# Output projection, h2 copies, last gates and samples' transposes moved in a one-layer decoder step

## The chip, the cores and the metric

The kernel runs on one core of one Trainium2 chip. The metric is the device time of one execution in microseconds (us), lower is better. The engines are TensorE (PE; PEld is its weight load), VectorE (DVE), ScalarE (ACT), GpSimd (POOL) and SyncE (SP), which here only issues transfers.

## What is computed

One decoder layer for 576 tokens: 512 of a prompt and 8 samples of 8 tokens, with a model width of 2048.

```python
mod = (jax.nn.silu(c) @ w_ada + b_ada).reshape(c.shape[0], 6, D_MODEL)
shift1, scale1, gate1, shift2, scale2, gate2 = [mod[:, k] for k in range(6)]
h = modulate(rmsnorm(x, norm1_g), shift1, scale1)
proj = h @ w_in                       # 2048 -> x_lru | y_gate | B | C | x_sc, 1024 each
...
xc, new_lru_buf = causal_dwconv(x_lru, lru_buf, lru_conv_w)
rec, h_last = rglru(xc + lru_conv_b, h0, lru_wa, lru_ba, lru_wx, lru_bx, lru_lambda)
out_lru = rec * jax.nn.gelu(y_gate)
conv_out, new_sc_buf = causal_dwconv(sc_c * sc_x, sc_buf, sconv_w)
out_sc = sc_b * conv_out
mix = jnp.concatenate([rmsnorm(out_lru, gnorm_lru_g), rmsnorm(out_sc, gnorm_sc_g)], axis=-1) @ w_out
x = x + gate1[:, None, :] * mix
h2 = modulate(rmsnorm(x, norm2_g), shift2, scale2)
x = x + gate2[:, None, :] * peer(h2, peer_wq, peer_sub_keys, peer_u, peer_v)
...                                   # then a final RMSNorm
```

`peer` is a product-key layer: 8 heads score 128 x 128 keys, each token takes the 16 best of 16384 single-neuron experts for each head, and the sum of their outputs, weighted by a softmax, is added.

## The kernel before

Everything is kept with channels on the partitions: a tensor of width 2048 is 16 blocks `k` of 128 channels by 576 tokens, and a matmul takes the tokens in two halves of 288 (`HT`). All large products are made in three parts, to come near full precision: an operand is split into a high part (`hi`, a rounding copy on ScalarE) and a low part (`lo`, the difference, on VectorE or GpSimd), and high x high, high x low and low x high are added up. `hv[0]` and `hv[1]` are the split activations, first of h, later of the mixers' outputs, later of h2. Weights are streamed by halves of 8 blocks, with two buffers each for the raw, high and low form; the low form of the weights is made on GpSimd. One projection of 128 output channels (`project`, `mm3`) is 16 blocks x 3 parts x 2 halves = 96 matmuls into a pair of PSUM banks; there are two such pairs (tag `pp`).

The first stage works in this order. The adaLN modulation is computed by units of 4 matmul calls (`ada_mm`, profile line L185; `ada_out`, L195), which `ada_turn` strews between projections. The head of group A has 8 mixers `i` (128 channels each): projections x and y, convolution, two gate products (`lru_gate(i, 0)` and `lru_gate(i, 1)`, L431, tiles `pg`, made into `tr` and `ti` by ScalarE), the scan (`lru`, `gate`). Then the square sums of group A (`sqa_g`, tag L216), projections c, s and b of the 8 mixers of group B (`pp_c`, `pp_s`, `pp_b`), each with its follow-up on ScalarE or VectorE (`sc_c`, `sc_x` at L482 to L491, `sc_b` at L497 to L499). `norm_stats` sums the squares over the channels on TensorE (L224, tile `pc_g`) and makes the factors on VectorE (L139 to L145, tile `rc_g`); `spread` puts them on all partitions by TensorE (L232, `st_g`). Group A's outputs are scaled (L545) and split while group B is still worked on; group B's are scaled at L557 and split at L241 and L242 (`hhi`, `hlo`). Then come the 16 projections of `w_out` (`pp_o`), the residual x1 and the statistics of x1 (`pc_n`).

h2 is made in four quarters of 4 blocks. For each quarter: `modulate` (multiply on VectorE or GpSimd, high part on ScalarE at L270, low part on VectorE at L271), 24 matmuls of the first query projection (`qa`), and 32 matmuls that transpose the quarter back to tokens on the partitions (L608, tile `wide`, four PSUM banks), which ScalarE copies to `h2s` (L611) for a store to `h2d`. The next query projection takes one of the first three banks of `wide`.

In this first stage TensorE's order is the order of the program. The orders of the other engines are set by a planner when the program is built; `tc.high_priority()` raises what stands in it ahead of other work that is ready. Later, from the last query head on, every engine keeps the order of the program.

Then come the query projections, the choice of experts, and two long loops on TensorE over the 84 most used key rows: the U loop (L1270) and the V loop (L1290; 84 steps of 4 columns `kq`, 12 matmuls a column). The experts outside those rows are gathered by row on GpSimd's queue and summed on VectorE (L1159, L1185), and their sums stored to `accd`. `finish_b` finishes the 64 sample tokens in six pieces, which `fplan` puts at places (step, column) in the V loop: load of the samples' rows (`tokb`, L1346, and `x2b`); transposes on TensorE (`ph`, L1353) with the residual behind them; sum of squares; statistics; spreading; last multiplication and store of the samples' y (L1364). `last` is step 75 of 84. At step 79 the prompt's rows (`tok`) are loaded, which the last four steps transpose and add (L1294). In the V loop SP also loads weight blocks of a later step (L831) and blocks of x (`xf`, L1301).

Of the kernel before, what the change touches and what calls it, by code (L numbers as in the profile page):

```python
# [21 lines left out]
HT = T // 2  # L22
NCTX = 1 + NB
W = 1024
KW = 8
# [47 lines left out]
def r32(ap):  # L73
    return ap.bitcast(F32)


def build(ctx, tc, A, O, dbg=None):
    nc = tc.nc
    V, S, PE, G = nc.vector, nc.scalar, nc.tensor, nc.gpsimd
# [4 lines left out]
    ws = ctx.enter_context(tc.tile_pool(name="ws", bufs=1))  # L84
# [24 lines left out]
    def lo_engine(share):  # L109

        turn[0] += 1
        return G if turn[0] * share // 8 != (turn[0] - 1) * share // 8 else V

    def stream_w(src, nm, share=8):
        his, los = [], []
        for hf in range(2):
            raw = ws.tile([128, 8, 128], F32, name=f"raw_{nm}_{hf}", tag="wraw", bufs=2)
            nc.sync.dma_start(raw, src[:, 8 * hf:8 * hf + 8, :])
            hi = ws.tile([128, 8, 128], F32R, name=f"whi_{nm}_{hf}", tag="whi", bufs=2)
            S.activation(hi, raw, AF.Copy)  # L120
            lo = ws.tile([128, 8, 128], F32R, name=f"wlo_{nm}_{hf}", tag="wlo", bufs=2)
            lo_engine(share).tensor_sub(lo, raw, r32(hi))  # L122
            his.append(hi)
            los.append(lo)
        return his, los

    def mm3(outs, his, los, movs, ks=range(KD)):

# [111 lines left out]
    def split(hi, lo, src, eng=V):  # L240
        S.activation(hi, src, AF.Copy)  # L241
        eng.tensor_sub(lo, src, r32(hi))  # L242
# [135 lines left out]
    o = big.tile([128, KD, T], F32, name="o", tag="big")  # L378

    def project(src, nm):  # L380
        his, los = stream_w(src, nm)
        p = pp.tile([128, 2, 512], F32, name=f"pp_{nm}", tag="pp")
        mm3([p[:, 0, :HT], p[:, 1, :HT]], his, los, movs)
        return p
# [39 lines left out]
    def lru_gate(i, j):  # L424
        xc = xcs[i]
        hl = LN // 2
        dst, g, hc = (wt("tr", i), gw[0], i) if j == 0 else (wt("ti", i), gw[1], KW + i)
        for q in range(2):
            pg = pst.tile([128, 512], F32, name=f"pg{i}_{hc}_{q}", tag="st")
            for z in (slice(0, 64), slice(64, 128)):  # L430
                PE.matmul(pg[z, :hl], g[z, i, :], xc[z, q * hl:(q + 1) * hl], start=True, stop=True)  # L431
            S.activation(dst[:, q * hl:(q + 1) * hl], pg[:, :hl], AF.Tanh, scale=0.5, bias=hb[:, hc:hc + 1])
        gts[i, j] = dst
# [26 lines left out]
    def gate_act(i, halves):  # L460
        ygs[i] = wk.tile([128, T], F32, name=f"yg{i}", tag="yg", bufs=2)
        for a, p in enumerate(halves):
            S.activation(ygs[i][:, a * HT:(a + 1) * HT], p, AF.Gelu_apprx_tanh)
# [8 lines left out]
    def sc_c(i, p):  # L472
        c = wk.tile([128, T], F32, name=f"scc{i}", tag="yg", bufs=2)
        S.activation(c.rearrange("p (a b) -> p a b", a=2), p[:, :, :HT], AF.Copy)
        sc_t[i] = c
# [28 lines left out]
    def ada_turn(n, keep=7):  # L504

        for a in pend:
            ada_out(*a)
        pend.clear()
        for _ in range(min(n, len(todo) - keep)):
            a = todo.pop(0)  # L510
            ada_mm(*a)
            if a[2] == 3:
                pend.append(a[:2])
                break
# [4 lines left out]
    for i in range(KW):  # L519
        if i + 1 < KW:  # L520
            lru_conv(i + 1, px)
        if i + 2 < KW:
            px = project(A["w_in"][i + 2], f"x{i + 2}")
            ada_turn(1)
        lru_gate(i, 0)
        if i + 1 < KW:
            py = project(A["w_in"][KW + i + 1], f"y{i + 1}")
            gate_act(i + 1, [py[:, a, :HT] for a in range(2)])
        lru_gate(i, 1)
        lru(i)  # L530
        gate(i)
        ada_turn(1)
    st = []
    for i in range(KW):
        square_sum(o[:, i, :], i, st, "g0")
    for i in range(KW):
        sc_c(i, project(A["w_in"][24 + i], f"c{i}"))
        if i == 0:
            spread = norm_stats(st, W, "g0")
        ada_turn(2)  # L540
        if i == 0:
            R = spread()
            st = []
            for k in range(KW):
                V.scalar_tensor_tensor(o[:, k, :], o[:, k, :], cols[:, C_GN + k:C_GN + k + 1], R, op0=ALU.mult, op1=ALU.mult)  # L545
        sc_x(i, project(A["w_in"][32 + i], f"s{i}"))
        ada_turn(2)
        sc_b(i, project(A["w_in"][16 + i], f"b{i}"))
        ada_turn(2)
        square_sum(o[:, KW + i, :], i, st, "g1")  # L550
    for k in range(KW):
        split(hv[0][:, k, :], hv[1][:, k, :], o[:, k, :], G if k % 2 else V)
    spread = norm_stats(st, W, "g1")
    ada_turn(2)
    R = spread()
    for k in range(KW, KD):
# [9 lines left out]
    st = []  # L566
    g1 = mods[2]
    for k in range(KD):
        p = project(A["w_out"][k], f"o{k}")
        xk = wk.tile([128, T], F32, name=f"xk{k}", tag="yg", bufs=2)  # L570
        nc.sync.dma_start(xk, A["xt"][:, k, :])
        V.scalar_tensor_tensor(x1[:, k, :HT], p[:, 0, :HT], g1[:, k, 0:1], xk[:, :HT], op0=ALU.mult, op1=ALU.add)
        V.scalar_tensor_tensor(x1[:, k, HT:NP], p[:, 1, :NX], g1[:, k, 0:1], xk[:, HT:NP], op0=ALU.mult, op1=ALU.add)
        V.tensor_tensor(s3(x1[:, k, NP:]), s3(p[:, 1, NX:HT]), ctx_b(g1, k), op=ALU.mult)
        V.tensor_add(x1[:, k, NP:], x1[:, k, NP:], xk[:, NP:])
        nc.sync.dma_start(x1d[:, k, :], x1[:, k, :])
        square_sum(x1[:, k, :], k, st, "n2")
        S.activation(x1[:, k, :NP], x1[:, k, :NP], AF.Copy, scale=mods[4][:, k, 0:1])
        V.tensor_tensor(s3(x1[:, k, NP:]), s3(x1[:, k, NP:]), ctx_b(mods[4], k), op=ALU.mult)
        ada_turn(1)  # L580
# [21 lines left out]
    for q in range(4):  # L602
        modulate(x1, R, 4, 3, 4 * q, 4, "h2")
        mm3(pq0, *w_q, movs, range(4 * q, 4 * q + 4))
        for i in range(NA // 128):
            for k in range(4):
                for p in range(2):
                    PE.matmul(wide[:, i, k * 128:(k + 1) * 128], hv[p][:, 4 * q + k, i * 128:(i + 1) * 128], idr,  # L608
                              start=p == 0, stop=p == 1)
        t = adap.tile([128, 4, 512], F32, name=f"h2s{q}", tag="wa")  # L610
        S.activation(t, wide, AF.Copy)  # L611
        for i in range(NA // 128):
            nc.sync.dma_start(h2d[i * 128:(i + 1) * 128, q * 512:(q + 1) * 512], t[:, i, :])
    pe1.close()
# [968 lines left out]
            room[m, kq] = PIECE / 2 - 0.75 * steps[m][4] - 0.38  # L1583
    tot, run_ = sum(room.values()), 0.0
    fb = finish_b()
    fplan = {(last + 1, 2), (last + 2, 0), (last + 2, 2), (last + 2, 3), (last + 3, 1), (last + 3, 3)}
    NT = len(uses)
    cost = [FULL_ROWS if j < NU + bound[0] else 1.0 for j in range(NV0, NT)]
    sums = [sum(cost[:j + 1]) for j in range(len(cost))]
# [189 lines left out]
```

## Time and profile before

| | |
|---|---|
| time, median of 3 runs | 3421.0 us (3416.03 to 3427.66) |
| profiled execution | 3418.08 us, of which the span of its instructions 3416.3 us |
| granted TensorE clock, mean | 0.961 |
| TensorE busy | 3196.4 us (94%) |
| VectorE busy | 2164.3 us (63%) |
| ScalarE busy | 1083.4 us (32%) |
| GpSimd busy | 1752.5 us (51%) |
| DMA | 868.17 MB, mean 254 GB/s |

A row of the groups or of the order of time names line, engine, operation, tiles (written<-read) and count; what stands in square brackets or behind an arrow is the idle time of that engine just before, and what ended it. A row of the waits gives the total in us, how often, and the longest. A row of the stretches gives for each engine the busy us and the number of instructions.

### The profile page before, as it was taken

The numbers are of one execution on the slowest core, as the hardware profiler recorded it, in microseconds if no ns is written. First come the engines' busy times: TensorE is split into PE (matmuls) and PEld (weight loads), VectorE is DVE, ScalarE is ACT, GpSimd is POOL, SyncE is SP. The second block draws the span as 40 slices with busy tenths as digits, with TensorE's granted clock in tenths as the row PEclk, the third lists the DMA queues.
The fourth block names the chain that finished last, engine by engine and source line by source line (L and its number), as shares of the span: only waits on it lengthen the run. The fifth ranks groups of instructions, "written<-read, shape, count | busy, mean of one in ns | idle before, by whom it ended". The sixth has DMA issues, their size and how long they took to land.

```text
span 3416.3 us, 47510 instructions
## 1 busy us (share of the span) xinstructions
PE 3196.4 (94%) x17641; PEld 2710.3 (79%) x17641; DVE 2164.3 (63%) x3246; ACT 1083.4 (32%) x1665; POOL 1752.5 (51%) x993
## 2 busy tenths in 40 slices
PE   5899999989979999989999999998999999999887
PEld 2698788989969988878888888876888777777776
DVE  5355522143346887968786787766677777787735
ACT  3234311132232232315555555522322222222122
POOL 4233233344333336646555566566767766676742
PEclk8899999999989999989999999998999999999988
DMA  9644466634442137759986979899999988898954
GB/s 337 231 139 139 160 208 205 216 114 128 130 138 71 66 102 255 263 186 366 340 302 259 376 284 370 317 365 334 369 386 368 368 297 330 301 393 297 337 170 148
DMA packets 304029, 868.17 MB, mean 254 GB/s; under 512 B 36618, under 2 KB 80522, under 8 KB 255658
## 3 DMA queue, kind: packets, MB, share of 16 engines
q1 hardware_dynamic: 165152, 390.35, 33.5%
q0 software_dynamic: 62896, 386.64, 29.0%
q10 hardware_dynamic: 75744, 88.09, 7.3%
q8 instruction: 139, 2.28, 0.3%
q14 instruction: 98, 0.80, 0.1%
HBM read 864.69 MB, written 68.90 MB: 273 GB/s over the span
## 4 chain that ended last, share of the span: by engine, by line
PE 39%; DMA 9%; DVE 8%; issue 5%; POOL 3%; ACT 0%; SPq 0%; POOLq 0%; ACTq 0%; DVEq 0%
PE pu L1270 19%; PE pv L1290 15%; PE gbank L1463 3%; DMA v<-v,rows 3%; DMA gsb<-gd 2%; DMA actr<-actd 2%; DVE u L1159 2%; DVE accB L1185 2%; DMA raw<-v 1%; POOL xlo L843 1%; DVE flags L1000 1%; POOL u L1131 1%; DMA h2r<-h2d,tok 0%; DVE oh L728 0%; PE pv L1294 0%
## 5 line engine op out<-in xcount | busy, mean ns | idle before, releaser
L843 POOL TENSOR_TENSOR xlo<-raw,xhi 128x1024 fp32r<-128x1024 f32 x336 | 818.4, 2447 | 643.9 <-ACT xhi L842 637.0
L842 ACT ACTIVATE xhi<-raw 128x1024 fp32r<-128x1024 f32 x336 | 354.1, 1059 | 922.9 <-PE pv L1290 466.1
L1159 DVE SCALAR_TENSOR_TENSOR u<-u,hT 128x2048 f32<-128x2048 f32 x211 | 479.5, 2284 | 242.5 <-DMA u<-u,rows 242.0
L1185 DVE SCALAR_TENSOR_TENSOR accB<-v,dots,accB 128x2048 f32<-128x2048 f32 x205 | 482.4, 2353 | 156.3 <-DMA v<-v,rows 154.5
L1290 PE MATMUL pv<-ahi,xhi 128*128 128x512 f32 x1344 | 540.9, 402 | 31.3 <-DVE acc L1312 24.2
L1290 PE MATMUL pv<-ahi,xlo 128*128 128x512 f32 x1344 | 538.3, 401 | 17.0 <-POOL xlo L843 16.9
L1270 PE MATMUL pu<-hhi,xhi 128*128 128x512 f32 x1344 | 543.4, 404 | 4.3 <-ACT xhi L842 4.3
L1270 PE MATMUL pu<-hhi,xlo 128*128 128x512 f32 x1344 | 529.8, 394 | 7.5 <-POOL xlo L843 7.5
L1290 PE MATMUL pv<-alo,xhi 128*128 128x512 f32 x1344 | 534.8, 398 | 0.0
L1270 PE MATMUL pu<-hlo,xhi 128*128 128x512 f32 x1344 | 531.4, 395 | 0.0
L1290 PEld LDWEIGHTS pv<-ahi,xhi 128*128 128x128 f32 x1344 | 257.8, 192 | 93.1 <-issue 16.7
L1290 PEld LDWEIGHTS pv<-ahi,xlo 128*128 128x128 f32 x1344 | 257.3, 191 | 82.8 <-POOL xlo L843 22.8
L1270 PEld LDWEIGHTS pu<-hhi,xlo 128*128 128x128 f32 x1344 | 254.8, 190 | 67.8 <-POOL xlo L843 10.4
L1290 PEld LDWEIGHTS pv<-alo,xhi 128*128 128x128 f32 x1344 | 258.0, 192 | 58.6
L1270 PEld LDWEIGHTS pu<-hhi,xhi 128*128 128x128 f32 x1344 | 255.6, 190 | 57.5 <-ACT xhi L842 5.6
L1270 PEld LDWEIGHTS pu<-hlo,xhi 128*128 128x128 f32 x1344 | 255.5, 190 | 50.1
L1131 POOL DMA_INDIRECT v<-v,rows x211 | 249.2, 1181 | 58.3 <-issue 32.5
L1131 POOL DMA_INDIRECT u<-u,rows x211 | 221.3, 1049 | 72.1 <-DVE u L1159 32.3
L1457 ACT ACTIVATE op<-op,it 128x128 f32<-128x128 f32 x512 | 154.3, 389 | 0.0
L185 PE MATMUL ada<-wa,cpad 128*32 128x512 f32 x768 | 112.5, 691 | 42.9 <-DMA wa<-w_ada 42.9
L1463 PEld LDWEIGHTS gbank<-wr,op 128*128 128x128 f32 x1024 | 135.5, 193 | 18.7 <-ACT op L1457 8.0
L122 POOL TENSOR_TENSOR wlo_q<-raw_q,whi_q 128x1024 fp32r<-128x1024 f32 x28 | 67.4, 2407 | 146.1 <-ACT whi_q L120 146.1
(477 smaller groups left out, 5574.9 us busy)
## 6 DMA issues: line engine op xcount, KB each, us to landing
wa<-w_ada SPq DMA_DIRECT2D x96, 1024.0 KB, 6.4
raw<-ut SPq DMA_DIRECT2D x168, 512.0 KB, 5.8
raw<-v SPq DMA_DIRECT2D x336, 256.0 KB, 8.0
actd<-act ACTq DMA_DIRECT2D x84, 256.0 KB, 7.1
gd<-stg ACTq DMA_DIRECT2D x64, 336.0 KB, 8.8
actr<-actd ACTq DMA_DIRECT2D x21, 1024.0 KB, 21.3
gsb<-gd ACTq DMA_DIRECT2D x21, 1024.0 KB, 26.2
raw_o<-w_out SPq DMA_DIRECT2D x32, 512.0 KB, 3.8
```

Of the source, the lines that this page charges most:

```text
L122: lo_engine(share).tensor_sub(lo, raw, r32(hi))
L185: PE.matmul(acc[32 * g:32 * g + 32, :], cpad[:, 4 * kq + g, :], w[:, g, :], start=kq == 0, stop=kq == 3)
L842: S.activation(hi, raw, AF.Copy)
L843: G.tensor_sub(lo, raw, r32(hi))
L1000: V.scalar_tensor_tensor(fl, i1, perm[:, x:x + 1], fl, op0=ALU.is_equal, op1=ALU.add)
L1131: G.indirect_dma_start(out=out, out_offset=None, in_=src, in_offset=bass.IndirectOffsetOnAxis(ap=idx, axis=0), bounds_check=NE * 128 - 1, ...
L1159: V.scalar_tensor_tensor(r, r, 1.0, st["h"], op0=ALU.mult, op1=ALU.mult, accum_out=dots[i][:, j:j + 1])
L1185: V.scalar_tensor_tensor(st["a"], r, dots[i][:, j:j + 1], st["a"], op0=ALU.mult, op1=ALU.add)
L1270: PE.matmul(pu, st[:, kk, :], movA[mv](k), start=k == 0 and a == 0, stop=k == KD - 1 and a == 2)
L1290: PE.matmul(pv, st, mv, start=first and j == 0 and a == 0, stop=last and not end and j == SG - 1 and a == 2)
L1457: S.activation(ops[:, j0 + j, :], ops[:, j0 + j, :], AF.Copy, scale=it[2][:, b * 4 + j:b * 4 + j + 1])
L1463: PE.matmul(pg[:, j * L:(j + 1) * L], ops[:, j0 + j, :], wr[:, j0 + j, :], start=True, stop=True)
```

## The change

Four places are changed.

1. The last mixer of group A: between its two gate products now stand an adaLN unit and projection c0. In group B, every projection s now comes directly after c and one adaLN turn; the statistics of group A, which stood behind c0, now stand behind s0.
2. The first two output projections are made by halves. The halves over group A's blocks (`out_half(0, 0)`, `out_half(1, 0)`) now stand ahead of the statistics of group B and between them and the spreading; the halves over group B's blocks follow when the loop over `w_out` comes to them. `half_w` is the half of `stream_w`, taken out of it.
3. The copy of the transposed h2 is made by pairs of PSUM banks, each after its 16 matmuls, under `tc.high_priority()`, instead of all four banks after 32.
4. In `fplan` the second to the sixth piece of the samples' end are moved: (last + 2, 0) to (last + 2, 3), (last + 2, 2) to (last + 3, 1), (last + 2, 3) to (last + 3, 3), (last + 3, 1) to (last + 4, 1), (last + 3, 3) to (last + 4, 3).

```diff
+    def half_w(src, nm, hf, share=8):
+        raw = ws.tile([128, 8, 128], F32, name=f"raw_{nm}_{hf}", tag="wraw", bufs=2)
+        nc.sync.dma_start(raw, src[:, 8 * hf:8 * hf + 8, :])
+        hi = ws.tile([128, 8, 128], F32R, name=f"whi_{nm}_{hf}", tag="whi", bufs=2)
+        S.activation(hi, raw, AF.Copy)
+        lo = ws.tile([128, 8, 128], F32R, name=f"wlo_{nm}_{hf}", tag="wlo", bufs=2)
+        lo_engine(share).tensor_sub(lo, raw, r32(hi))
+        return hi, lo
...
             gate_act(i + 1, [py[:, a, :HT] for a in range(2)])
+        else:
+            ada_turn(1)
+            pc0 = project(A["w_in"][24], "c0")
         lru_gate(i, 1)
         lru(i)
         gate(i)
-        ada_turn(1)
+        if i + 1 < KW:
+            ada_turn(1)
...
-        sc_c(i, project(A["w_in"][24 + i], f"c{i}"))
+        sc_c(i, project(A["w_in"][24 + i], f"c{i}") if i else pc0)
+        ada_turn(2)
+        sc_x(i, project(A["w_in"][32 + i], f"s{i}"))
         if i == 0:
             spread = norm_stats(st, W, "g0")
         ada_turn(2)
...
-        sc_x(i, project(A["w_in"][32 + i], f"s{i}"))
-        ada_turn(2)
         sc_b(i, project(A["w_in"][16 + i], f"b{i}"))
...
+    def out_half(k, hf):
+        hi, lo = half_w(A["w_out"][k], f"o{k}", hf)
+        mm3([p_out[k][:, i, :HT] for i in range(2)], (hi, hi), (lo, lo), movs, range(8 * hf, 8 * hf + 8))
+
+    p_out = [pp.tile([128, 2, 512], F32, name=f"pp_o{k}", tag="pp") for k in range(2)]
+    out_half(0, 0)
     spread = norm_stats(st, W, "g1")
+    out_half(1, 0)
     ada_turn(2)
     R = spread()
...
-        p = project(A["w_out"][k], f"o{k}")
+        if k < 2:
+            out_half(k, 1)
+            p = p_out[k]
+        else:
+            p = project(A["w_out"][k], f"o{k}")
...
+        t = adap.tile([128, 4, 512], F32, name=f"h2s{q}", tag="wa")
         for i in range(NA // 128):
             for k in range(4):
                 for p in range(2):
                     PE.matmul(wide[:, i, k * 128:(k + 1) * 128], hv[p][:, 4 * q + k, i * 128:(i + 1) * 128], idr,
                               start=p == 0, stop=p == 1)
-        t = adap.tile([128, 4, 512], F32, name=f"h2s{q}", tag="wa")
-        S.activation(t, wide, AF.Copy)
+            if i % 2:
+                with tc.high_priority():
+                    S.activation(t[:, i - 1:i + 1, :], wide[:, i - 1:i + 1, :], AF.Copy)
...
-    fplan = {(last + 1, 2), (last + 2, 0), (last + 2, 2), (last + 2, 3), (last + 3, 1), (last + 3, 3)}
+    fplan = {(last + 1, 2), (last + 2, 3), (last + 3, 1), (last + 3, 3), (last + 4, 1), (last + 4, 3)}
```

More of the change, by code (lines that the diff above doesn't have):

```diff
@@ L114, in stream_w @@
     def stream_w(src, nm, share=8):
[L115 to L124, printed above, removed]
-        return his, los
+        his, los = zip(*[half_w(src, nm, hf, share) for hf in range(2)])
+        return his, los
+    def half_w(src, nm, hf, share=8):
[6 more added lines that the diff above has]
+        return hi, lo
     def mm3(outs, his, los, movs, ks=range(KD)):
```

## The prediction, made before the changed kernel was run

> **What bounds the kernel now.** I read the page first, then TensorE's waits, then the busy time of each engine over short stretches, then the order of instructions inside those stretches.
>
> ```profile
> PE 3196.4 (94%) x17641; PEld 2710.3 (79%) x17641; DVE 2164.3 (63%) x3246; ACT 1083.4 (32%) x1665; POOL 1752.5 (51%) x993
> ```
>
> TensorE is busy 94% of the span and its instructions run in the order in which they are written, so an edit gains what it takes out of TensorE's idle time and out of the slow clock that follows idle time. The waits of TensorE in the first stage, between 357 and 1019.5 us, longest first (total, times, longest):
>
> ```profile
> PE wide L608 <- ACT h2s L611: 9.0, 1, 9.0
> PE pc_g L224 <- DVE sqa_g L216: 8.7, 2, 6.8
> PE pg L431 <- ACT tr L432: 5.1, 1, 5.1
> ...
> PE wide L135 <- ACT h2s L611: 2.0, 1, 2.0
> PE pp_o L135 <- POOL hlo L242: 1.9, 1, 1.9
> PE st_g L232 <- DVE rc_g L145: 1.5, 1, 1.5
> PE ada L185 <- DMA wa<-w_ada: 1.3, 1, 1.3
> ```
>
> The change touches `pg`, both `pc_g`, `st_g`, `pp_o` and both `wide` rows: 28.2 us. The stretches where they lie: from mixer 7's first gate to projection s0, from b7 to the last split of group B, from the first quarter's transposes of h2 to the next query projection, and, near the end, from V step 76 to its neighbour's last column. PEclk is the granted clock, the counts beside PE are of matmuls:
>
> ```profile
> core 0: us, PE busy (x) PEld busy (x) DVE busy (x) ACT busy (x) POOL busy (x), PEclk, DMA share, GB/s
> 357.10:387.00 29.90, 23.05 (x148) 17.67 (x149) 18.65 (x29) 9.45 (x16) 7.57 (x3) 0.83 0.37 123
> 728.30:756.40 28.10, 17.61 (x110) 17.05 (x110) 21.49 (x27) 8.83 (x14) 9.44 (x5) 0.80 0.15 50
> 982.50:1018.70 36.20, 25.24 (x168) 24.86 (x167) 12.12 (x13) 14.86 (x16) 20.04 (x13) 0.76 0.33 111
> 3272.00:3297.20 25.20, 18.22 (x70) 15.57 (x69) 6.94 (x6) 3.27 (x3) 4.27 (x2) 0.66 0.40 101
> 383.60:387.00 3.40, 3.40 (x18) 2.13 (x11) 0.67 (x4) 0.61 (x2) 0.15 (x1) 0.50 0.65 196
> 3303.50:3325.80 22.30, 22.30 (x98) 18.16 (x98) 9.36 (x9) 4.47 (x5) 9.06 (x5) 1.00 0.82 260
> ```
>
> In the first four rows TensorE stands still for 6.9, 10.5, 11.0 and 7.0 us, and the granted clock is 0.66 to 0.83. The last row is the same engine undisturbed: clock 1.00, 22.30/98 = 0.228 us a matmul. So a wait costs itself and then work at half clock. The four parts of the change answer to the first four rows in order.
>
> **The last gates behind a projection.** For mixer 7 the two gate products stood one behind the other; now one adaLN unit and projection c0 stand between them.
>
> ```profile
> 355.83 1.23 PE L431 MATMUL pg<-xc,g_lru_wa 64*64 64x300 f32 x8 [0.96 <-ACT ti L432]
> 362.14 2.27 PE L431 MATMUL pg<-xc,g_lru_wx 64*64 64x300 f32 x8 [5.08 <-ACT tr L432]
> 364.34 1.94 PE L185 MATMUL ada<-wa,cpad 128*32 128x512 f32 x8
> ...
> 381.21 1.28 PE L224 MATMUL pc_g<-ones,sqa_g 128*128 128x1 f32 x10 [1.81 <-DVE sqa_g L216]
> 382.42 2.52 PE L185 MATMUL ada<-wa,cpad 128*32 128x512 f32 x16
> ```
>
> Between the end of `ada` (366.28) and the idle time before `pc_g` (379.40) lies c0: 13.1 us for 96 matmuls, 0.137 each. Moved ahead of the second gate, it covers the 5.08 us wait for `tr`. The squares then have s0 (another 13.1) to arrive in, so the 1.81 before `pc_g` goes as well. With them goes slow clock: the second gate's 2.27 against 1.23 (1.0), 8 adaLN matmuls in 1.94 where 16 take 2.52 (0.7), half of the 3.4 us at 0.50 (1.7). That is 10.3. The moved adaLN unit takes its weight load ahead of c0's on SP's queue; that costs nothing while loads run ahead (the last row of the waits: 1.3 us in the whole stage), and 1.3 if not.
>
> What is late next: s0 now comes before the statistics, and its follow-up on VectorE is written ahead of theirs.
>
> ```profile
> 400.09 0.46 DVE L482 TENSOR_TENSOR cx<-pp_s,scc 128x288 f32<-128x288 f32 x1 [6.44 <-PE pp_s L135]
> ...
> 403.88 1.71 DVE L491 SCALAR_TENSOR_TENSOR cv<-cx,cols,cv 128x592 f32<-128x592 f32 x2
> ```
>
> It lasts 5.5 us (400.09 to 405.59). From the end of s0, TensorE has `pc_g` (1.3) and 16 adaLN matmuls (2.5), then wants the factors: at 3.8. If they queue behind the 5.5 and then need their own 1.5 (the `st_g` row), they come at 7.0: a new wait of 3.2, with all of b0 behind it, and 1.7 to 3.4 of slow clock. Part: 10.3 - 3.2 - 3.4 = 3.7 to 10.3; I take 6, near the queued case, as VectorE keeps its order.
>
> The Trainium skill's page "TensorE: Matmul & The Clock Gate", section "HAM oscillation — how this bites in real kernels", lets only idle gaps over about 3.4 us throttle the clock; here 1.81 us was followed by 3.4 us at 0.50, so the trace doesn't bear the limit out. By that rule the 3.2 us would cost no clock and this part would be 7.1, 1 us more than taken.
>
> **Output projection begun with the first mixer.** Two half projections, 96 matmuls, move ahead of and behind group B's square statistics; the sum of the work is unchanged.
>
> ```profile
> 729.17 3.56 DVE L242 TENSOR_TENSOR hlo<-o,hhi 128x576 fp32r<-128x576 f32 x2
> ...
> 741.82 2.28 DVE L557 SCALAR_TENSOR_TENSOR o<-o,cols,R_g 128x576 f32<-128x576 f32 x3 [2.91 <-ACT R_g L236]
> 744.01 1.42 DVE L242 TENSOR_TENSOR hlo<-o,hhi 128x576 fp32r<-128x576 f32 x2
> ...
> 750.05 4.82 DVE L557 SCALAR_TENSOR_TENSOR o<-o,cols,R_g 128x576 f32<-128x576 f32 x2
> ```
> ```profile
> 749.81 2.57 POOL L122 TENSOR_TENSOR wlo_o<-raw_o,whi_o 128x1024 fp32r<-128x1024 f32 x1 [3.09 <-ACT whi_o L120]
> 752.34 1.92 POOL L242 TENSOR_TENSOR hlo<-o,hhi 128x576 fp32r<-128x576 f32 x1
> ```
>
> Before: the second split on GpSimd (ends 754.26) is of k = 13, which TensorE waits for after 13 x 6 + 2 = 80 matmuls; the 112 left of o0 and o1 end at 754.3 + 15.3 = 769.6. After: the first half (48 x 0.137 = 6.6) starts at 728.3, the last of its splits is there at 732.7, so it ends about 734.9, just as `pc_g` could start before (728.3 + 6.8). `pc_g` to 736.2, the second half to 742.8, the spreading about 1.3 (10 short matmuls, by the 2.52 of 16 above), and the scaling of group B starts at about 744.7 instead of 741.8: the factors are 2.9 later. From there VectorE needs between 10.3 us (8 scalings of 0.76, 6 splits of 0.71, the undisturbed rows) and what it took before, about 14.5 (741.82 to the splits behind 754.87). The last split is done at 755.0 to 759.2; one k of matmuls (0.8) and the last half projection (6.6) end at 762.4 to 766.6, a gain of 3.0 to 7.2. TensorE idles three to four microseconds before k = 8, so up to 3.4 of slow clock falls into the last half: 0 to 7. Against the better end: the second half frees a weight buffer at 742.8, so a weight subtraction of 2.57 on GpSimd runs into the first scaling. I take 3.
>
> That GpSimd stalls VectorE is in the rows: two scalings took 4.82 us under GpSimd's 2.57 + 1.92, three took 2.28 with it idle. "SBUF — State Buffer" of the Trainium skill, section "Who interferes with whom", gives the cause, an exclusive port pair, and this trace agrees; it speaks against this part, since by it the fast end (7.2) isn't to be had.
>
> **The h2 copies by pairs of banks.** Four copies of four banks become eight of two, written ahead in priority.
>
> ```profile
> 989.50 0.71 ACT L270 ACTIVATE hhi<-m_h,mod 128x512 fp32r<-128x512 f32 x1
> 992.15 0.72 ACT L270 ACTIVATE hhi<-m_h,mod 128x512 fp32r<-128x512 f32 x1 [1.94 <-POOL m_h L269]
> 992.78 1.86 ACT L611 ACTIVATE h2s<-wide 128x2048 f32<-128x2048 f32 x1
> ```
> ```profile
> 1001.50 2.38 POOL L122 TENSOR_TENSOR wlo_q<-raw_q,whi_q 128x1024 fp32r<-128x1024 f32 x1
> ```
>
> The first copy had its transposes at about 982.5, but stood in ScalarE's queue behind the high parts of k = 12 and 13. TensorE did its 24 matmuls of the second quarter (3.3) and then stood for the 9.0. A pair is ready two microseconds earlier than all four banks, so I put its copy behind k = 12 (990.2 + 0.9 = 991.1) and the other behind k = 13: TensorE goes on 3.5 us sooner. The 2.0 before the next query projection goes too, which needs only a bank of the first pair, and about 1.7 of the clock lost behind it: 7 in all. If the queue stays as it is, half a copy (0.9) and the 2.0 are left: 3. If the copies pass the whole queue, the next bound is the weight part at 1003.88, without which the next projection (1018.7 before) cannot start: 15.
>
> **The samples' transposes later.** `ph` moves behind three columns of the V loop (36 matmuls), the later steps with it.
>
> ```profile
> 3279.00 7.09 PE L1353 MATMUL ph<-ident,tokb 64*128 64x64 f32 x32 [6.98 <-DMA tokb<-accd]
> ```
> ```profile
> 3274.18 0.54 SPq L1346 DMA_DIRECT2D tokb<-accd x1
> ```
> ```profile
> DMA to landing us min/median/max: 4.8/4.8/4.8
> ```
>
> The rows it needs land at 3274.18 + 4.8 = 3278.98. Three columns from 3272.0 take 36 x 0.228 = 8.2, so `ph` starts at 3280.2, 1.2 us after the landing: the 6.98 goes. So does slow clock: up to half of the 7.09, and of the stretch's other 38 matmuls (18.22 - 7.09 = 11.1 us) what 38 x 0.228 = 8.7 leaves, 2.5. Together 7.0 + 3.5 + 2.5 = 13; I take 12, since these short matmuls need not double in speed. If the rows land later beside other traffic, or clock is lost at the next wait, 6 is left. The samples' store moves on SP behind the loads of the token rows and ahead of a load of x and the last weight blocks; they have three V steps of cover, 36 us, and if SP stands there for the multiplication, two or three of it are used.
>
> **Sum.** 6 + 3 + 7 + 12 = 28 us; ends 3.7 + 0 + 3 + 6 = 13 and 10.3 + 7.2 + 15 + 13 = 46. The profiled execution took 3418.1 us (span 3416.3) and would take 3390; it lies 2.9 under the median of the three times shown, 3421.0, so on that footing the forecast is 3393.
>
> **The rivals.** *The h2 queue stays as it is.* Priority decides only among what the planner holds for ready, and it put the first copy behind k = 13 although it is written before k = 4. Part three is then 3: 3397. *Given back.* Up to the query stage an earlier TensorE may meet a later ScalarE or GpSimd, their order being the planner's; only the last part, whose order is fixed by hand, is left: 3421 - 12 = 3409. Against it: the waits named are each ended by one chain that starts earlier too. *Slower.* The priority puts the copies ahead of the next quarter's high parts. ScalarE then stands until TensorE has transposed, and TensorE waits for the high parts behind it: a quarter is 24 matmuls at half clock (6.6), its transposes at half clock (about 7, as 36.2 - 25.2 idle and 0.76 of clock leave them now) and 3 of waiting (copy 0.95, high part 0.72, low part about as long, and the hand-overs), some 17; the three that are left at 982.5 end at 1033 instead of 1018.7, 14 lost. It decides once a copy stands before the high parts of the quarter that follows it; in the trace it stood ten places behind that. With parts one and two spent by the same planner: 3421 + 14 - 12 = 3423, and 3432 with the last part at its low end (6) and part two 3 below nothing (a second weight subtraction in the scalings).
>
> **How the numbers follow.** Forecast as summed 0.6, queue as it is 0.17, given back 0.13, slower 0.1. About 0.3%, 10 us, is what a measurement of this kernel can tell from no change. The first two lie beyond it; given back lies on its edge (3410.7) and is split evenly, the slower case, 3423 to 3432, too. Faster 0.6 + 0.17 + 0.06 = 0.83, same 0.07 + 0.05 = 0.12, slower 0.05. The range runs from the sum of the good ends (3421 - 46 = 3375) to the given-back case, with the 3 us by which the times shown scatter at either end: 3372 to 3412; the likeliest case alone is 3376 to 3405.
>
> **What would show it.** Right: no wait at the second gate of mixer 7; `pp_o` between b7 and `pc_g`; eight h2 copies of about 0.95 us; `ph` without a wait and clock 1.00 around it. Each of the four stretches should end earlier by its term. A wait of about 3 us at `st_g` before b0, and one before k = 8 in the output projection, should be new. Wrong: `wide` still waiting 6 us or more after the first quarter, `ph` still waiting for its rows, or a shift won by 1019 us that is gone when the V loop starts.

## The result, and the profile after

The changed kernel takes 3399.3 us (median of 7 runs, 3396.94 to 3407.14) beside 3422.1 for the kernel before (7 runs, 3416.03 to 3433.95). The ratio is 0.9936, interval [0.9919, 0.9954]: by it 21.9 us less, 15.7 to 27.7. The forecast was 3393 with 3372 to 3412.

The profiled execution of after is the slowest of its seven (3407.14 us, span 3405.3), so the pair of profiles shows 11 us, not 22. The stages explain that. First the busy time over four stretches with the same marks in both kernels: mixer 7's projection y to projection b0; b7's end to the end of the output projections; the start of h2 to the next query projection; V step 72 to the end. Columns as in the stretches above; the kernel before first.

```profile
339.07:402.27 63.20, 55.34 (x390) 45.67 (x388) 41.55 (x66) 21.41 (x31) 15.07 (x7) 0.92 0.41 134
728.03:950.42 222.39, 211.90 (x1559) 211.13 (x1557) 83.71 (x113) 60.41 (x74) 85.78 (x38) 0.97 0.37 117
965.80:1018.73 52.93, 36.52 (x244) 34.34 (x236) 27.62 (x36) 21.99 (x28) 27.18 (x17) 0.77 0.27 94
3214.55:3416.28 201.73, 164.47 (x757) 135.88 (x755) 109.00 (x108) 42.03 (x50) 72.71 (x35) 0.89 0.53 180
```

The same four stretches of the changed kernel:

```profile
336.92:392.57 55.65, 51.63 (x390) 44.15 (x389) 38.38 (x64) 23.06 (x31) 16.24 (x7) 1.00 0.52 171
718.24:934.86 216.62, 211.06 (x1559) 209.60 (x1557) 84.17 (x113) 60.55 (x74) 85.53 (x38) 0.98 0.37 120
951.50:1006.08 54.58, 39.06 (x245) 36.27 (x237) 26.42 (x36) 22.54 (x32) 26.67 (x17) 0.80 0.26 91
3214.52:3405.26 190.74, 161.84 (x757) 133.64 (x755) 106.09 (x108) 41.58 (x50) 74.68 (x35) 0.91 0.56 189
```

Stretches one, two and four shrink by 7.5, 5.8 and 11.0 us; the third, that of the h2 copies, grows by 1.7. In the first, 3.8 us of TensorE's idle time go (7.86 to 4.02, length less busy) and 3.7 us of busy time: the granted clock rises from 0.92 to 1.00.

TensorE's waits in the first stage of the changed kernel, which answer to the rows of before (total, times, longest):

```profile
PE wide L625 <- ACT h2s L629: 9.0, 5, 4.2
...
PE pp_o L135 <- ACT hhi L241: 4.0, 2, 3.6
...
PE st_g L232 <- DVE rc_g L145: 2.7, 1, 2.7
...
PE wide L135 <- ACT h2s L629: 1.1, 1, 1.1
PE pp_o L135 <- DVE hlo L242: 1.1, 2, 0.8
...
PE pc_g L224 <- DVE sqa_g L216: 0.4, 1, 0.4
```

The rows that the change touches fell from 28.2 to 18.3 us. `pg` behind `tr` (5.1) is gone, `pc_g` fell from 8.7 to 0.4. `wide` kept its 9.0, only cut into five pieces. New are 3.6 at `pp_o` and 1.2 more at `st_g`.

The stages of all kernels that were run follow, each length the difference of two start times in its trace. "h2" goes from the first multiplication of h2 to the fifth query projection behind the transposes (four projections past the mark above), so that a wait that only moves into the next projections is seen. "V" is the V loop's first 72 steps.

| kernel | y7 to b7 | b7 to last o | h2 | V | V72 to end | ratio to before |
|---|---|---|---|---|---|---|
| before | 389.0 | 222.4 | 111.4 | 865.1 | 201.7 | 1 |
| after | 381.3 | 216.6 | 113.9 | 876.6 | 190.7 | 0.9936 [0.9919, 0.9954] |
| part_gates | 381.4 | 221.1 | 111.6 | 860.2 | 201.6 | 0.9986 [0.9971, 1.0001] |
| part_outproj | 388.3 | 216.7 | 111.8 | 867.6 | 201.2 | 0.9997 [0.9983, 1.0011] |
| part_h2 | 388.2 | 221.1 | 114.2 | 867.3 | 201.6 | 1.0002 [0.9988, 1.0016] |
| part_samples | 388.4 | 221.1 | 111.5 | 875.7 | 188.6 | 0.9970 [0.9956, 0.9984] |
| pair_tiles | 381.3 | 216.6 | 107.1 | 871.2 | 187.5 | 0.9938 [0.9920, 0.9955] |
| stats_first | 384.1 | 216.6 | 114.3 | 867.3 | 188.9 | 0.9949 [0.9931, 0.9967] |
| spread_early | 384.2 | 214.6 | 114.1 | 866.4 | 190.0 | 0.9948 [0.9930, 0.9965] |
| samples_later | 382.9 | 216.6 | 114.1 | 869.8 | 189.1 | 0.9935 [0.9914, 0.9956] |
| spread_late | 378.5 | 216.6 | 113.7 | 864.5 | 187.6 | 0.9934 [0.9917, 0.9951] |
| three_edits | 381.3 | 214.1 | 107.5 | 870.2 | 187.3 | 0.9896 [0.9871, 0.9921] |
| four_edits | 378.5 | 214.1 | 108.3 | 875.3 | 190.0 | 0.9876 [0.9854, 0.9897] |
| one_tile | 378.5 | 214.1 | 114.0 | 856.0 | 185.4 | 0.9925 [0.9907, 0.9942] |

From before to after the four changed stages sum to -7.7 - 5.8 + 2.5 - 11.0 = -22.0, about what the ratio shows. The V loop's 72 steps took 11.6 us more in the profile of after than in that of before; that hides half of it in this pair. It looks like scatter, although each kernel was profiled only once: the loop takes 856.0 to 876.6 us over these profiles, and `one_tile` with 856.0 and after with 876.6 run the same instructions over these steps, since the moved pieces all come later. The execution profiled of `one_tile` was also its fastest (3377.9, median 3392.6), that of after its slowest. The two ends of that spread, after's row first, then `one_tile`'s:

```profile
2337.89:3214.52 876.63, 826.78 (x3456) 663.52 (x3457) 636.18 (x367) 204.66 (x191) 599.10 (x355) 0.96 0.92 343
```
```profile
2334.60:3190.63 856.03, 817.99 (x3457) 659.07 (x3457) 638.12 (x367) 204.37 (x191) 598.28 (x355) 0.97 0.94 350
```

TensorE idles 49.9 us in the one and 38.0 in the other (length less busy) and is 8.8 us longer busy on the same matmuls.

### The profile page after: what moved, and what is told of

The parts are those of the page before. It is cut to its first block, busy times and chain, and to the rows that moved or that the text cites. A ratio compares the mean times of both kernels' runs of the same rounds, so it can differ in the third digit from the quotient of the medians.

```text
span 3405.3 us, 47522 instructions
## 1 busy us (share of the span) xinstructions
PE 3203.1 (94%) x17641; PEld 2712.2 (80%) x17641; DVE 2159.1 (63%) x3246; ACT 1086.2 (32%) x1671; POOL 1749.4 (51%) x993
## 3 DMA queue, kind: packets, MB, share of 16 engines
q8 instruction: 139, 2.28, 0.3%
## 4 chain that ended last, share of the span: by engine, by line
PE 37%; DMA 11%; DVE 8%; issue 4%; POOL 3%; ACT 0%; SPq 0%; POOLq 0%; ACTq 0%; DVEq 0%
PE pu L1288 19%; PE pv L1308 14%; DMA v<-v,rows 4%; PE gbank L1481 3%; DMA gsb<-gd 2%; DMA raw<-v 2%; POOL xlo L861 2%; DVE u L1177 2%; DMA actr<-actd 2%; DVE accB L1203 1%; DVE flags L1018 1%; POOL u L1149 1%; DMA h2r<-h2d,tok 0%; DVE oh L746 0%; PE pv L1312 0%
## 5 line engine op out<-in xcount | busy, mean ns | idle before, releaser
L861 POOL TENSOR_TENSOR xlo<-raw,xhi 128x1024 fp32r<-128x1024 f32 x336 | 827.7, 2474 | 647.5 <-ACT xhi L860 642.4
L1149 POOL DMA_INDIRECT v<-v,rows x211 | 236.2, 1120 | 60.3 <-issue 37.5
```

Of the source, the lines that this page charges most:

```text
L861: G.tensor_sub(lo, raw, r32(hi))
L1149: G.indirect_dma_start(out=out, out_offset=None, in_=src, in_offset=bass.IndirectOffsetOnAxis(ap=idx, axis=0), bounds_check=NE * 128 - 1, ...
```

## The experiments

### Each part alone

Each of these four kernels is the kernel before with one part of the change, as in the diff above. First the gates:

```diff
+        else:
+            ada_turn(1)
+            pc0 = project(A["w_in"][24], "c0")
         lru_gate(i, 1)
...
+        ada_turn(2)
+        sc_x(i, project(A["w_in"][32 + i], f"s{i}"))
         if i == 0:
             spread = norm_stats(st, W, "g0")
```

> Part 1 alone on the kernel before (second gate product of mixer 7 behind c0, group A's statistics behind s0). Theory: the stage is bound by TensorE's own order, so its gain is independent of the other parts: from the start of projection y7 to the start of b0 63.2 us before, 55.6 to 55.8 here as in the changed kernel, with a wait of about 2.7 us left at st_g; time 0.2% (7 us) under before. Rival (given back): the stage gains the 7.5 us but a later stage waits longer and the shift at the start of the V loop is under 3 us.

Measured: ratio 0.9986 [0.9971, 1.0001]; the stretch y7 to b7 is 381.4 beside 389.0 in before and 388.2 to 388.4 in the other three. The part is worth 6.8 to 7.6 us in its stage, all that after shows there. The rival can't be settled by one profile: from y7 to the start of the V loop this kernel takes 2003.7 us beside 2010.4, but `part_samples`, which changes nothing ahead of the V loop, takes 2003.8.

The output projection:

```diff
+    out_half(0, 0)
     spread = norm_stats(st, W, "g1")
+    out_half(1, 0)
...
+        if k < 2:
+            out_half(k, 1)
+            p = p_out[k]
```

> Part 2 alone on the kernel before (halves of the output projection around group B's statistics). Theory: from the end of b7 to the end of the last output projection 222.4 us before, 216.5 to 216.8 here, with a wait of 3.6 us before k = 8 that is ended by ScalarE's high part; time about 6 us under before, hard to tell from no change. Rival: the gain in the changed kernel needed part 1's orders on the other engines; alone it is under 3 us.

Measured: 0.9997 [0.9983, 1.0011]; b7 to the last o is 216.7, with the 3.6 us wait, beside 222.4 in before and 221.1 in the other three: 4.4 to 5.7 us.

The h2 copies:

```diff
-        S.activation(t, wide, AF.Copy)
+            if i % 2:
+                with tc.high_priority():
+                    S.activation(t[:, i - 1:i + 1, :], wide[:, i - 1:i + 1, :], AF.Copy)
```

> Part 3 alone on the kernel before (h2 copies by pairs, with priority). Theory: the pairs work in lockstep, each pair's transposes wait for the copy of the pair before; from R of h2 to the first query projection after h2 52.9 us before, 54 to 55.5 here, nine microseconds of waits at the transposes in five or six pieces instead of one; time 1 to 3 us over before, not to be told from no change. Rival: in the changed kernel the stage only fell badly against the clock's windows; alone it gains 3 to 7 us.

Measured: 1.0002 [0.9988, 1.0016]; the stage takes 114.2 beside 111.4 to 111.8, so the part costs 2.4 to 2.8 us there.

The samples:

```diff
-    fplan = {(last + 1, 2), (last + 2, 0), (last + 2, 2), (last + 2, 3), (last + 3, 1), (last + 3, 3)}
+    fplan = {(last + 1, 2), (last + 2, 3), (last + 3, 1), (last + 3, 3), (last + 4, 1), (last + 4, 3)}
```

> Part 4 alone on the kernel before (samples' transposes three columns later). Theory: from the start of V step 77 to the end of the kernel 144.3 us before, 133 to 136 here; time 9 to 11 us under before (0.3%). Rival: the shift is taken up by longer waits for the token rows (tok) in the last four steps: 139 us or more.

Measured: 0.9970 [0.9956, 0.9984], the only part whose own interval leaves 1 out; step 72 to the end is 188.6 beside 201.2 to 201.7, 13 us. Its `ph` waits 0.20 us, and the waits for `tok` are no longer than before (5.0 beside 5.3), so the rival is out.

The times of the four add up to 15 us less, those of the stages to 21 to 24; the intervals, about 5 us to either side each, do not let the times say more. The stages do: parts one, two and four act alone about as they act together, and so does the third, which loses.

### Two tiles for the transposes

In after, ScalarE's order over the first quarters shows where the copies stand:

```profile
967.58 0.72 ACT L270 ACTIVATE hhi<-m_h,mod 128x512 fp32r<-128x512 f32 x1 [1.50 <-DVE m_h L269]
968.71 0.72 ACT L270 ACTIVATE hhi<-m_h,mod 128x512 fp32r<-128x512 f32 x1 [0.41 <-DVE m_h L269]
969.34 0.40 ACT L241 ACTIVATE hhi<-ms_h 128x256 fp32r<-128x256 f32 x1
969.64 1.00 ACT L629 ACTIVATE h2s<-wide 128x1024 f32<-128x1024 f32 x1
...
977.35 1.34 ACT L270 ACTIVATE hhi<-m_h,mod 128x512 fp32r<-128x512 f32 x2 [2.08 <-POOL m_h L269]
978.59 1.00 ACT L629 ACTIVATE h2s<-wide 128x1024 f32<-128x1024 f32 x1
```

and TensorE's order what waits for them:

```profile
966.10 0.27 PE L625 MATMUL wide<-idr,hhi 128*128 128x128 f32 x1
970.69 0.48 PE L625 MATMUL wide<-idr,hhi 128*128 128x128 f32 x1 [4.21 <-ACT h2s L629]
...
979.64 0.33 PE L625 MATMUL wide<-idr,hhi 128*128 128x128 f32 x1 [0.76 <-ACT h2s L629]
```

The first pair's transposes end at 966.5. The second pair's go into two other banks, which nobody reads; yet they start when the copy of the first pair has ended (969.64 + 1.00). So it goes five times: at the second pair of every quarter, and at the first pair of the second quarter. The theory: both pairs lie in one tile, and a write to the tile waits for a read of it, whatever the banks. The test makes each pair a tile of its own:

```diff
-    wide = psum["p"].tile([128, 4, 512], F32, name="wide", tag="hT", bufs=1)
+    wides = [pwp.tile([128, 2, 512], F32, name=f"wide{j}", tag=f"wide{j}") for j in range(2)]
...
-                    PE.matmul(wide[:, i, k * 128:(k + 1) * 128], hv[p][:, 4 * q + k, i * 128:(i + 1) * 128], idr,
+                    PE.matmul(wides[i // 2][:, i % 2, k * 128:(k + 1) * 128], hv[p][:, 4 * q + k, i * 128:(i + 1) * 128], idr,
...
-                    S.activation(t[:, i - 1:i + 1, :], wide[:, i - 1:i + 1, :], AF.Copy)
+                    S.activation(t[:, i - 1:i + 1, :], wides[i // 2], AF.Copy)
```

> The changed kernel with the four banks of h2's transposes as two tiles of two banks instead of one tile of four (the later transposed-row tile moves to a pool of its own). Theory (lockstep through the shared tile): a pair's transposes wait for the other pair's copy only because both lie in one tile; with two tiles the waits at the transposes fall from 9.0 us in five pieces to under 4 and the stretch from R of h2 to the first query projection behind h2 from 54.6 to 44 to 49 us; time 5 to 10 us under the changed kernel. Rival (ScalarE's queue): the copies stand behind the next quarters' high parts anyway, the waits stay over 6 us and the stretch over 51.

Its waits and its stretch of h2:

```profile
PE wide L627 <- ACT h2s L631: 5.0, 1, 5.0
...
PE qa L135 <- ACT qt L886: 3.9, 1, 3.9
```
```profile
951.57:996.12 44.55, 34.56 (x245) 33.02 (x237) 28.75 (x36) 21.42 (x31) 27.24 (x17) 0.85 0.29 101
```

ScalarE's first copy stands where it stood, behind the same high parts, but the second pair's transposes no longer wait for it; they start before it does (TensorE's row first):

```profile
965.97 0.28 PE L627 MATMUL wide<-idr,hhi 128*128 128x128 f32 x1
```
```profile
969.42 1.00 ACT L631 ACTIVATE h2s<-wide 128x1024 f32<-128x1024 f32 x1
```

Four of the five waits are gone, the stretch takes 44.55 us instead of 54.58: the theory holds for the stage, although the 5.0 us left are more than the 4 it allowed. But a wait of 3.9 that after does not have follows in the second query projection, for a copy on ScalarE that itself stood 7.3 us, by the trace for the store of h2. Over four projections more, 6.8 of the 10 us are left (107.1 beside 113.9). The time did not show them: 3398.7 us, ratio 0.9938. `one_tile`, below, takes that up.

### What the factors of group A wait for

The prediction laid the wait at `st_g` to s0's follow-up, queued ahead of the statistics. `stats_first` writes it behind:

```diff
-        sc_x(i, project(A["w_in"][32 + i], f"s{i}"))
+        ps = project(A["w_in"][32 + i], f"s{i}")
         if i == 0:
             spread = norm_stats(st, W, "g0")
+        sc_x(i, ps)
```

> The changed kernel with s0's follow-up on VectorE written behind group A's statistics instead of ahead of them. Theory (VectorE's queue): the 2.7 us wait at st_g falls under 1, y7 to b0 from 55.7 to 53 us. Rival (the factors' own chain, with ScalarE's square root in it): the wait stays at 2 or more. No difference of the whole time that can be told.

The wait stayed (2.62 us), and the edit turned out to be no test: VectorE's order hardly changed. In after, VectorE did this,

```profile
386.01 2.22 DVE L486 COPY o_st_s<-cx 128x16 f32<-128x16 f32 x1
388.14 0.52 DVE L489 TENSOR_SCALAR cv<-cx,cols 128x592 f32<-128x592 f32 x1
388.69 0.83 DVE L491 SCALAR_TENSOR_TENSOR cv<-cx,cols,cv 128x592 f32<-128x592 f32 x1
389.44 0.30 DVE L197 TENSOR_REDUCE pms<-pm 128x36 f32<-128x144 f32 x1
389.66 0.82 DVE L491 SCALAR_TENSOR_TENSOR cv<-cx,cols,cv 128x592 f32<-128x592 f32 x1
390.40 0.18 DVE L141 RECIPROCAL rc_g<-rc_g 128x5 f32<-128x5 f32 x1
```

while the square root that the reciprocal needs was there at 387.28:

```profile
385.77 1.28 ACT L140 ACT_TABLE_LOAD   x1
387.07 0.21 ACT L140 ACTIVATE rc_g<-rc_g 128x5 f32<-128x5 f32 x1
```

In `stats_first` the last two lines read:

```profile
391.87 0.82 DVE L491 SCALAR_TENSOR_TENSOR cv<-cx,cols,cv 128x592 f32<-128x592 f32 x1
392.61 0.17 DVE L141 RECIPROCAL rc_g<-rc_g 128x5 f32<-128x5 f32 x1
```

So the reciprocal still stood behind most of the follow-up, although it is written ahead of it; that the planner moved what it held for ready ahead of a result that it expected late is likely, not shown. The rows bear the queue out (3.1 us between square root and reciprocal in after), but no run took the queue away.

Most of that queue is one small copy. The copy of 16 columns took 2.22 us in after and ended (388.23) when a weight subtraction on GpSimd ended (388.19):

```profile
385.83 2.36 POOL L124 TENSOR_TENSOR wlo_b<-raw_b,whi_b 128x1024 fp32r<-128x1024 f32 x1 [4.01 <-ACT whi_b L122]
```

In `stats_first` a copy of 2 columns met the subtraction (388.84 to 391.20) instead. It took 1.79 us, and the copy of 16 columns behind it 0.16:

```profile
389.44 1.79 DVE L485 COPY o_st_s<-cx 128x2 f32<-128x2 f32 x1
391.14 0.16 DVE L486 COPY o_st_s<-cx 128x16 f32<-128x16 f32 x1
```

So about 2 of the 2.7 us at `st_g` lie in a VectorE copy held up by GpSimd, which the prediction reckoned with in part two but not here; no run took it away alone. `spread_late` instead covers the wait, by projection b0:

```diff
         ada_turn(2)
+        pb = project(A["w_in"][16 + i], f"b{i}")
         if i == 0:
             R = spread()
...
-        sc_b(i, project(A["w_in"][16 + i], f"b{i}"))
+        sc_b(i, pb)
```

> The changed kernel, but group A's spreading (st_g) and the scalings behind it are written behind projection b0 instead of ahead of it, so 96 more matmuls (13 us) stand between the factors and the spreading. In the changed kernel the square root is done at 387.28 and its reciprocal starts at 390.40, behind five instructions of s0's follow-up on VectorE; TensorE waits 2.72 us. If that wait costs just itself: no wait at st_g, mixer 7's y to b7 takes 2.7 us less than 381.3, so 378.6, and the time is 3396.7 beside 3399.3. Rival: VectorE's 5.9 us of scalings, 13 us later, hold up the follow-up of b0 and what comes after; then a wait at a later pp or st row takes the 2.7 back and the stretch stays at 381.

The wait is gone and y7 to b7 takes 378.5 us, the 378.6 expected; nothing behind gave it back. In the time 2.8 us are too little to be seen (0.9934). Beside kernels in which slow clock followed the wait (384.2 in `spread_early`) it is 5.7.

### The new wait before k = 8, and the last 0.6 us of `ph`

`spread_early` puts the spreading after 24 of the second half projection's 48 matmuls, so that group B's factors come earlier:

```diff
-    out_half(1, 0)
+    rest = out_half(1, 0)
+    next(rest)
     ada_turn(2)
     R = spread()
+    list(rest)
```

> The changed kernel with group B's factors spread after the first 24 matmuls of the second half projection instead of after all 48. Theory (the late factors bound the last halves): the scaling starts 3.3 us earlier, the 3.6 us wait before k = 8 falls under 1, and from b7's end to the end of the last output projection 216.6 becomes 213 to 214. Rival (VectorE and GpSimd stall each other in the scalings and splits): the first wait goes, later ones come, 215.5 or more.

Its waits in the output projection:

```profile
PE pp_o L135 <- DVE hlo L242: 3.0, 1, 3.0
...
PE pp_o L135 <- ACT hhi L241: 0.5, 1, 0.5
```

The 3.61 became 0.5, but a wait of 3.0 for a low part came. The scalings do start 3.2 us earlier after b7's end, but the second three take 5.54 us instead of 3.43, with GpSimd busy beside them (1.82 and 2.87), which points to VectorE's chain of scalings and splits as the bound behind both. 2.0 us are left (214.6 beside 216.6), between theory and rival, and none of it is seen in the time.

`samples_later` moves the second and third piece by one column more:

```diff
-    fplan = {(last + 1, 2), (last + 2, 3), (last + 3, 1), (last + 3, 3), (last + 4, 1), (last + 4, 3)}
+    fplan = {(last + 1, 2), (last + 3, 0), (last + 3, 2), (last + 3, 3), (last + 4, 1), (last + 4, 3)}
```

> The changed kernel with the samples' transposes one column later again ((last + 3, 0)), the next pieces at (last + 3, 2), (last + 3, 3), (last + 4, 1), (last + 4, 3). Theory: the 0.64 us left of the wait and the slow clock behind it go, ph takes 3.6 to 4.5 us instead of 5.35, from V step 72 to the end 190.7 becomes 187 to 189. Rival: the slow clock there isn't due to that wait; ph still over 5, 190 or more.

`ph` no longer waits and takes 3.78 instead of 5.35 us. That the wait had cost the difference is not shown: in `pair_tiles` `ph` waits 0.67 us and takes 3.78 too, and here the granted clock is 0.57 in the 4 us behind `ph`, as in after. The end takes 189.1, but without this edit it was 187.5 to 190.7, and with it 185.4 to 190.0 in the kernels below: whether it is worth anything beyond `ph` stays open.

### The edits together

`three_edits` has `pair_tiles`, `spread_early` and `samples_later` in one kernel, `four_edits` also `spread_late`; `one_tile` is `four_edits` without the two tiles. Their edits are those above.

> The changed kernel with three edits together: the transposes of h2 in two PSUM tiles of two banks (alone: the stage 54.58 to 44.55 us), spreading after the first 24 matmuls of the second half projection (216.62 to 214.61), the samples' pieces one more column later (ph wait 0.64 to 0, 190.7 to 189.1). If the stages add up and the loops behind them do not answer: 10.0 + 2.0 + 1.6 = 13.6 us less than 3399.3, so 3385.7. Rival, the first stage does not carry through: pair_tiles alone gave 3398.67 against 3399.31, though its stage ended 10 us earlier; if what follows takes it back, only 0.6 + 2 + 1.6 are left, about 3395.

> three_edits and spread_late together. If all add up: 3385.7 - 2.7 = 3383.0. If only the edits outside the first stage's last third carry through: about 3393. The stage tables should show 378.6 for mixer 7's y to b7, 214.6, 44.6 and about 189.

> The kernel of four_edits without its edit of the h2 tiles: wide is one tile of four banks again. It tells whether the 10 us that the two tiles took out of the stage of h2 reach the end, which pair_tiles alone left open (3398.67 beside 3399.31). If they do, this runs at 3382.45 + 10 = 3392 (ratio 0.9905). If the query projections behind wait for them (a new wait of 3.9 us there), 3389 (0.9895). If nothing is left of them, 3382 to 3383 (0.9877). The stage of h2 shows 54.5 us and five waits of wide, 9.0 in all.

Measured: 3390.6 (0.9896), 3382.5 (0.9876) and 3392.6 us (0.9925). `three_edits` lies between its theory and its rival. `four_edits` beats both kernels: its interval [0.9854, 0.9897] lies below that of after. The stages that it shortens (2.8 + 2.5 + 5.6 + 0.7 = 11.6 by the table) explain only part of the 20 us (0.0060 of 3422) between the ratios, so that its time meets the 3383.0 summed for it is in part luck. Its waits show what it leaves:

```profile
PE wide L632 <- ACT h2s L636: 5.2, 1, 5.2
...
PE qa L135 <- ACT qt L891: 3.9, 1, 3.9
```

`one_tile` speaks to what `pair_tiles` left open: without the two tiles the ratio is 0.0049 higher, 17 us, with intervals that do not touch. Its stretch of h2 is back at 54.35 us with five waits (8.5 in all). Its time is the 3392 expected if the gain reaches the end, its ratio is not (0.9925 for 0.9905). So the gain seems to reach the end, but that is not shown. The stages give 5.7 us (114.0 less 108.3), one pair of times nothing and the other three times as much, and the second pair ran on two chips, each beside the kernel before. From y7 to the start of the V loop two tiles take 4.7 us less in the first pair (2001.0 to 1996.3) and 7.8 less in the second (1993.3 to 1985.5), but unchanged work differs by 6.6 there (`part_gates`, above).

## Why the prediction was right, and where it was not

**The sum.** 28 us were forecast and 21.9 came, inside the range. Two terms came above their size (by 1.7 and 2.8), one came 1.0 below, and the one that failed took 9.5 away. That the range held in spite of it is in part luck: it was wide, and two small terms made up for almost half. The rival "the h2 queue stays as it is" names 3397, nearer to 3399.3 than the 3393 of the forecast, but by a mechanism that did not occur. The 3376 to 3405 given for the likeliest case alone do not follow from its own ends, which make 3375 to 3408.

**Part one: 6 forecast, 7.7 measured.** The second gate of mixer 7 stands behind c0 without a wait, and the new wait at `st_g` came, 2.72 us for 3.2, behind the queue named, though most of it is a copy held up by GpSimd (above). What was over-priced is the slow clock after it. TensorE's order and the granted clock behind the wait in after:

```profile
391.43 1.16 PE L232 MATMUL st_g<-ident,rc_g 128*128 128x128 f32 x8 [2.72 <-DVE rc_g L145]
```
```profile
392.57:405.60 13.03, 13.03 (x103) 12.86 (x105) 5.92 (x8) 1.96 (x4) 2.39 (x1) 1.00 0.44 161
```

In three other kernels the same wait did cost clock, so the price is right in some profiles only (last section).

**Part two: 3 forecast, 5.8 measured (4.4 against the other three parts' 221.1).** The chain went as worked out: the scalings of group B start at 734.80, 16.6 us after b7's end (16.7 forecast), the last split is done 30.4 after it (27.0 to 31.2 forecast), and the new wait before k = 8 is there:

```profile
734.80 3.69 DVE L569 SCALAR_TENSOR_TENSOR o<-o,cols,R_g 128x576 f32<-128x576 f32 x3 [5.89 <-ACT R_g L236]
...
747.16 1.49 DVE L242 TENSOR_TENSOR hlo<-o,hhi 128x576 fp32r<-128x576 f32 x2
```
```profile
737.80 0.56 PE L135 MATMUL pp_o<-hhi,whi_o 128*128 128x288 f32 x2 [3.61 <-ACT hhi L241]
```

GpSimd's weight subtraction did run into the first scalings (three in 3.69 us, where 2.28 stood before). The 3 us taken allowed a little too much for this and the wait.

**Part three: 7 forecast, a loss of 2.5 measured. This is the step that failed.** It was put as: the copy of a pair stands behind k = 12, so "TensorE goes on 3.5 us sooner". The copy did move up in ScalarE's queue. But the step took for granted that TensorE may write two banks while the other two are copied, and with one tile it may not: a quarter's second pair waits for the copy of the first, and the second quarter's first pair waited for a copy too. One wait of 9.0 became five that sum to 9.0. Slow clock follows two of them (those that end at 970.69 and 983.40; the row 970.69 to 976.00 below), and the stage's busy time grows by 2.5 us (36.52 to 39.06). Even the low end (3, "the queue stays as it is") rested on the same assumption (the 2.0 before the next query projection fell only to 1.1), and the rival that was to make the part lose, ScalarE standing at a copy ahead of the high parts, is not what happened: the first copies stand behind the high parts, as the rows show. The prediction's own sign of this failure, `wide` still waiting 6 us or more after the first quarter, did not show it as worded: 4.2 of the 9.0 fell inside the first quarter and 4.8 after it. With two tiles the part gives 4.3 us (111.4 to 107.1), inside the 3 to 15. The slow clock behind the longest of the five waits:

```profile
970.69:976.00 5.31, 5.31 (x24) 5.31 (x25) 4.43 (x4) 1.75 (x3) 4.63 (x5) 0.50 0.26 99
```

**Part four: 12 forecast, 11.0 measured in after and 13.1 alone.** The wait of 6.98 fell to 0.64:

```profile
3279.15 5.35 PE L1371 MATMUL ph<-ident,tokb 64*128 64x64 f32 x32 [0.64 <-DMA tokb<-accd]
```

`ph` was to start 1.2 us after the landing; it started at it. Slow clock came with it (last section), against the 1.00 forecast around `ph`. The 1.0 us by which the part missed is less than the scatter of the stage: 187.5 to 190.7 over the six profiles with these places in `fplan`.

**Given back.** This rival is out: it leaves only the last part, 12 us forecast and 11.0 to 13.1 measured, and the measured gain is at least 15.7. That the four stages' net of 22.0 us meets the measured 21.9 so closely is chance, as part four's stage alone scatters by 3 us. What looked like giving back in the pair of profiles is the V loop's 11.6 us.

## What to carry to other kernels

A transfer cut into pieces overlaps only if the pieces are separate to whatever orders reads and writes: ask of each half copy whether the next write goes to the same tile, and give each half a tile of its own before pricing the gain. Writing an instruction earlier, or with priority, moves it only as far as the planner lets it; read the engine's order in the new trace before taking the run for a test. When one long stage scatters by more than the change is worth, compare the changed stages between fixed marks, and leave the total to many runs.

## What the runs showed of the hardware that was not expected

How long a wait is did not alone decide whether the clock falls behind it. Seven kernels have the same wait at the same place, `st_g` ahead of b0. In after, `part_gates`, `pair_tiles` and `three_edits` it was 2.71 to 2.72 us and the eight matmuls behind it took 1.16 us, at full clock (rows of after above). In `stats_first`, `spread_early` and `samples_later` it was 2.62 to 2.73 and the eight took 1.86 to 2.08. In `spread_early`, the wait and the clock behind it:

```profile
396.11 2.07 PE L232 MATMUL st_g<-ident,rc_g 128*128 128x128 f32 x8 [2.71 <-DVE rc_g L145]
```
```profile
396.90:401.00 4.10, 4.10 (x20) 4.10 (x19) 2.03 (x3) 0.71 (x2) 0.00 (x0) 0.50 1.01 370
```

That is why y7 to b7 is 381.3 or 381.4 in the one group and 382.9 to 384.2 in the other. At `ph` the clock did not follow the wait either. In after it fell to half behind a wait of 0.64 us, in `four_edits` behind none at all (no wait of TensorE shows in the 70 us before `ph`), and in `pair_tiles` it stayed full behind 0.67. The three in this order:

```profile
3282.00:3284.50 2.50, 2.50 (x13) 2.38 (x12) 0.00 (x0) 0.00 (x0) 0.00 (x0) 0.50 0.57 200
```
```profile
3270.18:3274.18 4.00, 4.00 (x11) 3.13 (x11) 2.80 (x3) 1.42 (x2) 0.09 (x1) 0.50 0.68 180
```
```profile
3273.39:3277.39 4.00, 4.00 (x18) 3.28 (x19) 2.80 (x3) 1.45 (x2) 0.00 (x0) 1.00 0.12 42
```

The limit of about 3.4 us of idle time that the Trainium skill gives ("TensorE: Matmul & The Clock Gate", section "HAM oscillation — how this bites in real kernels") fits the first group and not the second, nor `four_edits` at `ph`, where no wait went before. Its section "What's actually happening" calls the window by which the clock is set free-running; two outcomes of one wait would fit that, but no run here moved a wait against such a window, so what decides stays open. For the wait at `st_g` these profiles show slow clock worth nothing to 2.9 us.
